# Memory keys of a decoder block: two columns in parts against four columns in native fp32

## The chip, the cores and the metric

The kernel runs on one core of one Trainium2 chip. The metric is the device time of one execution in microseconds; a kernel is run several times and the median is taken. One execution was profiled, and every row below that begins with a time, an engine or a tile comes from its page or its trace.

## The reference

One layer of a decoder: an input projection that feeds a convolution branch and a sparse attention branch, then cross attention over 256 fixed memory tokens, then an MLP. The change touches the keys of the cross attention:

```
memn = _rmsnorm(mem, norm_mem_g)          # mem: 256 tokens x 1024
kv   = memn @ wx_kv                       # 1024 x (512 keys + 512 values)
k, v = jnp.split(kv, 2, axis=-1)          # k: 4 heads x 128
s    = jnp.einsum('bshd,bmhd->bhsm', q, k) * 128 ** -0.5
```

The per-token factor of the norm is applied later, to the scores; here the memory, transposed, is only multiplied by the gain `norm_mem_g`. All data are float32, x has 256 rows, and the model width is 1024, that is eight row tiles of 128 (kt 0 to 7).

## The kernel before

**Products in parts.** Nearly all products are made in parts: a float32 matrix is divided into `hi` (rounded to the fp32r type, by ACT) and `lo` (the rest, by DVE), and TensorE multiplies hi by hi, hi by lo and lo by hi in fp32r. A weight comes as a chunk of 128 x 2048 float32 (1 MB) in the order of the list `STREAM`; `load` issues its transfer on SP's queue, `split_high` and `split_low` take the next half chunk through `high` (ACT, `hi<-raw`) and `low` (DVE, `lo<-raw,hi`). Three buffers hold raw chunks; a new chunk is loaded when the parts of an old one are made. `tile_b` multiplies one column tile of a weight by x or memory; in its `wide` form hi meets both parts side by side (512 columns), then lo meets hi (256).

**A planner in the program.** `Counted` adds up a price of every instruction for TensorE, DVE and ACT. Where work is to be mixed, the generator compares these totals: taps of the convolution are filled into DVE (`meanwhile`, `tick`, `fill_one`) while DVE's total is less than 400 ns ahead of TensorE's (`AHEAD`). `may_fill` says when: with two or more lists of taps always, with one list while more than five tiles are done or while `nused[0] < 5`, the number of weight halves used so far. At the end of the opening all three totals are set to the largest of them.

**The opening**, which the change rewrites, in the order of the program:

- SP: the first half of memory (`mem_t`, row tiles 0 to 3, 512 KB), the first key column (`load_keys(0)`, 512 KB), the second half of memory, the second key column, then the two blocks of x (`x_rm`, 128 rows each) before the halves of the second key chunk (columns 2 and 3), then the first conv chunk in two halves, the conv taps `cw` and the second conv chunk. ACT's queue brings `vec`, the gains and biases.
- TensorE warms up with ten products of zeros, 128 x 512 (`ps_warm`).
- Memory is scaled by its gain on DVE, one instruction for each row tile. Columns 0 and 1 of the keys are multiplied natively in fp32 from the raw chunk, all eight row tiles of one column and then of the other. In between memory is also divided into parts (`mk2`: ACT `mk<-mem_t`, DVE `mk<-mem_t,mk`).
- `square_rows` takes the mean square of a block of x on ACT, a power on GpSimd, and scales the rows on DVE.
- Columns 2 and 3 are divided into parts and multiplied in the wide form, `tile_b(psk[0], ...)` and `tile_b(psk[1], ...)`. Between the two, TensorE transposes x, 16 products into four banks `pt_n` of PSUM (the tag `acc`, which has four).
- `scaled_parts` makes the parts of n out of these banks in the order `BY_BANK`: hi on ACT (`n<-pt_n,vec`), lo on DVE (`n<-pt_n,vec,n`).
- The finished keys are copied to `kx` by ACT; for columns 2 and 3 ACT copies one half of the bank and DVE adds the other (`total`).

Then `conv_in` begins. Its first tile takes a bank through `ps_turn`, whose first turn is the tag `acc`, that is the bank of the first transposes, row tiles 0 and 1:

```
BY_BANK = (0, 2, 4, 6, 1, 3, 5, 7)
tags, turns = [("mm", 2), ("acc", 4)], [0]
def ps_turn(name):
    turns[0] += 1
    tag, bufs = tags[turns[0] % len(tags)]
```

Later in the program memory is loaded once more and divided into parts for the values (`memory_parts`); that is not changed.

Of the kernel before, what the change touches and what calls it, by code (L numbers as in the profile page):

```python
# [8 lines left out]
F32 = mybir.dt.float32  # L9
# [7 lines left out]
P = 128  # L17
# [92 lines left out]
def block_kernel(ctx, tc, x, xt, mem, memt, wst, wki, vecs, convw, gout, out):  # L110
# [21 lines left out]
    def w2(name, dt=F32, shape=(P, 512)):  # L132
        return work.tile(list(shape), dt, tag="w2", bufs=8, name=name)
# [4 lines left out]
    def ps_mm(name):  # L138
        return bank("mm", 2, name)
# [53 lines left out]
    def load(cuts=(0, N_CHUNK), before=lambda q: None, second=False):  # L193
        if not any(by_blocks(key) == second for key in toload):
            return
        key = toload.pop(next(j for j, key in enumerate(toload) if by_blocks(key) == second))
        c = STREAM.index(key)
        raw = t8(f"raw{c}", F32, (P, N_CHUNK)) if c in EARLY or second else raws.tile([P, N_CHUNK], F32, tag="raw", name=f"raw{c}")
        n = KT * NK if key[0] == "ki" else N_CHUNK
        src = wki if key[0] == "ki" else wst[INDEX[key]]  # L200
        for q, ns in enumerate(slice(a, min(b, n)) for a, b in zip(cuts, cuts[1:])):
            before(q)
            nc.sync.dma_start(raw[:, ns], src[:, ns])
            dma[0] += 1.3 * (ns.stop - ns.start)
        if key[0] == "f2" and key[1] < SEVEN:
            seven_factors(key[1], c, raw, dma[0] + LANDED)
            return
        parts = 1 if key[0] == "ki" else 2
        turns = sorted(range(parts), key=lambda q: (*key, q) not in BY_DMA)
        for q in turns:  # L210
            ns = slice(q * n // parts, (q + 1) * n // parts)
            high_jobs.append((lambda ns=ns, q=q, last=q == turns[-1]: high(key, c, raw, ns, q, last), 1, 0, (lambda t=dma[0] + LANDED: t) if key[0] in ("f1", "f2") else None, c))

    def load_keys(q):
        if q == 0:
            toload.pop(0)
            whole["xk", 0] = raws.tile([P, N_CHUNK], F32, tag="raw", name="raw0").rearrange("p (k n) -> p k n", k=2 * KT)
        src = wst[INDEX["xk", 0]].rearrange("p (k n) -> p k n", k=2 * KT)
        nc.sync.dma_start(whole["xk", 0][:, q * KT : q * KT + KT, :], src[:, q * KT : q * KT + KT, :])

    def high(key, c, raw, ns, q, last):
        n = ns.stop - ns.start
# [91 lines left out]
    def split_low():  # L314
        if low_jobs:
            low_jobs.pop(0)()
# [95 lines left out]
    def split(hi, lo, src):  # L412
        act(hi, src, AF.Copy)
        dve.tensor_tensor(out=lo, in0=src, in1=hi.bitcast(F32), op=ALU.subtract)
# [67 lines left out]
    mem_t = t8("mem_t")  # L482
    x_rm = t8("x_rm", F32, (P, 2, D))

    def load_rows(q):
        nc.sync.dma_start(x_rm[:, q, :], x[q * P : (q + 1) * P, :])

    for q in range(2):
        ks = slice(4 * q, 4 * q + 4)
        nc.sync.dma_start(mem_t[:, ks, :], memt[:, ks, :])  # L490
        load_keys(q)
    load((0, 1024, 2048), load_rows)
    load((0, 1024, 2048))
    nc.sync.dma_start(cw, convw.rearrange("p (k t) -> p k t", k=KT))
    load()
    zero = w2("zero")
    nc.vector.memset(zero, 0.0)
    zero_r = cst.tile([P, 512], F32R, name="zero_r")
    nc.vector.tensor_copy(zero_r, zero)
    ident = cst.tile([P, P], F32, name="ident")  # L500
    make_identity(nc, ident)
# [8 lines left out]
    nc.scalar.activation(half, half, AF.Sigmoid, bias=0.0, scale=0.0)  # L510
    nc.gpsimd.memset(half, -0.5)
    ps = ps_aux("ps_warm")
    for j in range(10):
        nc.tensor.matmul(ps, zero_r[:, :P], zero_r, start=True, stop=True)


    def power(ms, name):
# [35 lines left out]
    ss = small.tile([P, 2], F32, tag="ss", name="ss_n")  # L553
    ptn = [ps_acc(f"pt_n{c}") for c in range(4)]

    mk2 = Pair("mk")
    psk = [ps_mm(f"ps_xk0{ct}") for ct in range(2)]
    for ct in range(2):
        for q in range(2):
            for kt in range(4 * q, 4 * q + 4):  # L560
                if ct == 0:
                    dve.tensor_scalar(mem_t[:, kt, :], mem_t[:, kt, :], g_mem[:, kt : kt + 1], None, ALU.mult)
                pe.matmul(psk[ct][:, :S], whole["xk", 0][:, ct * KT + kt, :], mem_t[:, kt, :], start=kt == 0,
                          stop=kt == KT - 1)
            if ct == 0:
                for kt in range(4 * q, 4 * q + 4):
                    split(mk2.hi(kt), mk2.lo(kt), mem_t[:, kt, :])
    load()

    def square_rows(rb):  # L570
# [5 lines left out]
        dve.tensor_scalar(x_rm[:, rb, :], x_rm[:, rb, :], rs[:, 0:1], None, ALU.mult)  # L576

    square_rows(0)
    split_high()
    split_low()  # L580
    square_rows(1)
    for ct in range(2):
        act(kx[:, ct, :], psk[ct][:, :S], AF.Copy)
    split_high()
    split_low()
    psk = [ps_aux(f"ps_xk1{ct}") for ct in range(2)]
    nused[0] += 1
    keys = [[w.rearrange("p (k n) -> p k n", k=KT) for w in prepared.pop(("xk", 1, ct))] for ct in range(2)]
    tile_b(psk[0], keys[0], mk2, wide=True)
    for rb in range(2):  # L590
        for kt in range(KT):
            pe.transpose(ptn[kt // 2][:, (kt % 2) * S + rb * P : (kt % 2) * S + rb * P + P],
                         x_rm[:, rb, kt * P : kt * P + P], ident)
    tile_b(psk[1], keys[1], mk2, wide=True)
    split_high()
    split_low()
    for kt in BY_BANK:
        scaled_parts(n2.hi(kt), n2.lo(kt), ptn[kt // 2][:, (kt % 2) * S : (kt % 2) * S + S], g_mix[:, kt : kt + 1])
    nused[0] += 1
    split_high()  # L600
    split_low()
    for ct in range(2):
        total(kx[:, 2 + ct, :], psk[ct])
    while due:
        due.pop(0)()
    split_high()
    pe.total = dve.total = scalar.total = max(pe.total, dve.total, scalar.total)

# [1033 lines left out]
```

## Time and profile before

| | us |
|---|---|
| median of 3 runs | 503.18 (502.93 to 508.85) |
| profiled execution | 502.87 |
| its span | 500.9 |
| TensorE busy | 490.9 (98%) |
| DVE busy | 456.0 (91%) |
| ACT busy | 384.8 (77%) |
| granted TensorE clock | 0.996 of full, mean |

The span begins with the first instruction and ends with the last. In the rows, PE is TensorE's products, PEld its weight loads, DVE, ACT and POOL the other engines, SPq the queue of transfers that SP issues. A timeline row has start, duration, engine, line, operation, output<-input, shapes and count; in brackets the idle time ahead of it and what ended it. A row of transfers has their count, size and the median time from issue to landing. `L91` is the line of the planner's wrapper, so most instructions have it, and tiles tell them apart.

### The profile page before, as it was taken

Reading aid. Unit: us, or ns where it says so; the run is one execution under the profiler, and the core shown is the slowest. Engines: PE = TensorE matmul, PEld = TensorE weight load, DVE = VectorE, ACT = ScalarE, POOL = GpSimd, SP = SyncE. Lnnn points to the kernel's source line nnn. Section 1 sums busy time; section 2 is a strip of 40 time slices with the busy share of each in tenths; the row PEclk is TensorE's granted clock in tenths of the full one; section 3 lists DMA queues with packets and bytes.
Section 4 is the critical chain, followed back from the end, with each engine's and each line's share of the span. In section 5 each row is a group of like instructions: output and inputs, shape, how many; then the busy total and the mean of one; then the engine's idle time right before and its main releaser. Section 6 shows DMA issues by size and latency. Waiting matters only on the chain.

```text
span 500.9 us, 8179 instructions
## 1 busy us (share of the span) xinstructions
PE 490.9 (98%) x3024; PEld 439.8 (88%) x3024; DVE 456.0 (91%) x835; ACT 384.8 (77%) x678; POOL 54.2 (11%) x75
## 2 busy tenths in 40 slices
PE   7999999999999999999999999999999999999994
PEld 6999999888888989888888888998888888889983
DVE  4889999999999999798999995789899999999996
ACT  4877667878879986888667575597889989899763
POOL 0101122233232210000000000000000010000000
PEclk9999999999999999999999999999999999999998
DMA  8968959999999984373756454665868779788502
GB/s 303 388 270 243 259 146 234 228 250 246 315 287 254 266 219 148 129 298 116 261 183 230 138 198 169 253 252 127 287 195 231 212 221 329 198 264 249 169 0 84
DMA packets 22342, 110.81 MB, mean 221 GB/s; under 512 B 2592, under 2 KB 3104, under 8 KB 11936
## 3 DMA queue, kind: packets, MB, share of 16 engines
q1 hardware_dynamic: 14384, 92.98, 52.7%
q0 software_dynamic: 7632, 17.04, 18.6%
q8 instruction: 23, 0.38, 0.3%
q10 hardware_dynamic: 288, 0.28, 0.2%
q14 instruction: 15, 0.12, 0.1%
HBM read 92.21 MB, written 1.05 MB: 186 GB/s over the span
## 4 chain that ended last, share of the span: by engine, by line
PE 88%; DVE 5%; ACT 3%; DMA 1%; issue 1%; SPq 0%; DVEq 0%; ACTq 0%
PE ps_f L91 14%; PE ps_ff L91 11%; PE ps_conv L91 9%; PE ps_ao L91 4%; PE ps_mix L91 4%; PE ps_co L91 4%; PE ps_ga L91 4%; PE ps_k L91 4%; PE ps_gc L91 4%; PE ps_q L91 4%; PE ps_v L91 4%; PE ps_xo L91 3%; PE ps_xq L91 2%; PE ps_qi L91 2%; PE ps_xk L91 2%; PE ps_xv L91 2%
## 5 line engine op out<-in xcount | busy, mean ns | idle before, releaser
L91 DVE TENSOR_TENSOR lo<-raw,hi 128x1024 fp32r<-128x1024 f32 (+1 forms) x151 | 174.7, 1166 | 8.0 <-ACT hi L91 8.0
L91 ACT ACTIVATE hi<-raw 128x1024 fp32r<-128x1024 f32 (+1 forms) x163 | 161.5, 1011 | 9.6 <-DMA raw<-in_wst_dram 6.1
L91 PE MATMUL ps_f<-ff,hi 128*128 128x256 f32 (+1 forms) x432 | 84.2, 303 | 0.0
L91 PEld LDWEIGHTS ps_f<-ff,hi 128*128 128x128 f32 x432 | 70.9, 191 | 4.4
L91 DVE SCALAR_TENSOR_TENSOR acc<-u,cw,acc 128x249 f32<-128x249 f32 (+17 forms) x150 | 62.6, 467 | 0.0
L91 PE MATMUL ps_f<-ff,lo 128*128 128x256 f32 x256 | 61.0, 283 | 0.0
L675 POOL DMA_DIRECT2D added<-prod x41 | 35.7, 870 | 120.5 <-ACT prod L91 52.7
L91 PE MATMUL ps_conv<-n,hi 128*128 128x256 f32 x256 | 46.6, 284 | 0.0
L91 PEld LDWEIGHTS ps_f<-ff,lo 128*128 128x128 f32 x256 | 44.6, 191 | 0.8
L91 PEld LDWEIGHTS ps_conv<-n,hi 128*128 128x128 f32 x256 | 39.9, 192 | 0.8 <-issue 0.7
L91 DVE TENSOR_TENSOR raw<-raw 128x512 f32<-128x512 f32 (+1 forms) x42 | 36.4, 867 | 0.9
L91 PE MATMUL ps_ff<-th,fs 128*128 128x512 f32 x112 | 36.9, 391 | 0.0
L91 PE MATMUL ps_ff<-hi,fs 128*128 128x512 f32 (+1 forms) x116 | 36.6, 377 | 0.0
L91 PE MATMUL ps_conv<-n,lo 128*128 128x256 f32 x128 | 36.2, 283 | 0.0
L91 ACT ACTIVATE prod<-u,cw 128x226 f32<-128x226 f32 (+10 forms) x82 | 35.0, 475 | 0.8 <-DMA added<-prod 0.8
L91 DVE TENSOR_TENSOR tl<-raw,th 128x1024 fp32r<-128x1024 f32 x28 | 33.2, 1219 | 1.2 <-ACT th L91 1.2
L91 ACT ACTIVATE th<-raw 128x1024 fp32r<-128x1024 f32 x28 | 28.3, 1052 | 1.7 <-DVE raw L91 1.7
L229 POOL DMA_DIRECT2D lo<-raw x12 | 10.4, 866 | 167.1 <-ACT lo L91 110.6
L91 ACT ACTIVATE ft<-ps_f 128x256 f32<-128x256 f32 (+1 forms) x32 | 14.4, 449 | 15.5 <-PE ps_f L91 15.5
L91 PEld LDWEIGHTS ps_ff<-th,fs 128*128 128x128 f32 x112 | 21.1, 188 | 4.2
L91 PEld LDWEIGHTS ps_ff<-hi,fs 128*128 128x128 f32 x116 | 21.4, 189 | 3.6
L91 PEld LDWEIGHTS ps_conv<-n,lo 128*128 128x128 f32 x128 | 24.5, 192 | 0.0
(262 smaller groups left out, 1039.2 us busy)
## 6 DMA issues: line engine op xcount, KB each, us to landing
raw<-in_wst_dram SPq DMA_DIRECT2D x79, 1024.0 KB, 6.2
added<-prod POOLq DMA_DIRECT2D x41, 256.0 KB, 7.7
lo<-raw POOLq DMA_DIRECT2D x12, 512.0 KB, 9.3
raw<-in_wst_dram SPq DMA_DIRECT2D x6, 512.0 KB, 9.3
mem_t<-in_memt_dram SPq DMA_DIRECT2D x2, 512.0 KB, 5.4
x_rm<-in_x_dram SPq DMA_DIRECT2D x2, 512.0 KB, 9.0
mem_rm<-in_mem_dram SPq DMA_DIRECT2D x1, 1024.0 KB, 5.0
mem_t<-in_memt_dram SPq DMA_DIRECT2D x1, 1024.0 KB, 7.0
```

What stands on the lines that cost most here:

```text
L91: return fn(*args, **kwargs)
L229: nc.gpsimd.dma_start(lo.bitcast(F32), raw[:, ns], accum_op=ALU.add)
L675: nc.gpsimd.dma_start(added[:, ts, :].rearrange("p t n -> p (t n)"), prod[:, self.n, :, :].rearrange("p t n -> p (t n)"), accum_op=ALU.add)
```

## The change

`load_keys` takes a column and a range of row tiles instead of a column, and the opening becomes:

- SP: thirteen pieces for memory and all four key columns, 256 KB each but for the first column's low rows, which come as two of 128 KB. The low row tiles (0 to 3) of all columns come first, memory in four pieces among them, then the high row tiles of columns 0 and 1, the two blocks of x, and the high row tiles of columns 2 and 3. The conv chunks and `cw` follow as before.
- Memory is scaled, all eight row tiles, and is not divided into parts. The second key chunk is not divided either.
- TensorE multiplies natively: low rows of columns 0, 1, 2, 3, high rows of columns 0, 1, 2, then the transposes of x, then the high rows of column 3. Columns 2 and 3 use the two `aux` banks.
- ACT copies all four columns to `kx`; the copy of column 2 and `split_high` for the second half of the first conv chunk stand ahead of the parts of n.
- `nused` is not counted up for the second key chunk any more.
- The warm-up is 19 products of 128 x 256, from tiles of zeros of that width.

```diff
-    def load_keys(q):
-        if q == 0:
+    def load_keys(ct, ks):
+        i, ct = divmod(ct, 2)
+        if ("xk", i) not in whole:
             toload.pop(0)
...
+        ks = slice(ct * KT + ks.start, ct * KT + ks.stop)
+        nc.sync.dma_start(whole["xk", i][:, ks, :], src[:, ks, :])
...
-    for q in range(2):
-        ks = slice(4 * q, 4 * q + 4)
+    def load_memory(ks):
         nc.sync.dma_start(mem_t[:, ks, :], memt[:, ks, :])
-        load_keys(q)
-    load((0, 1024, 2048), load_rows)
+
+    low_rows, high_rows = slice(0, 4), slice(4, 8)
+    load_memory(slice(0, 2))
+    load_keys(0, slice(0, 2))
+    load_keys(0, slice(2, 4))
+    load_memory(slice(2, 4))
+    load_keys(1, low_rows)
+    load_keys(2, low_rows)
+    load_memory(slice(4, 6))
+    load_keys(3, low_rows)
+    load_memory(slice(6, 8))
+    for rb in range(2):
+        load_keys(rb, high_rows)
+    for rb in range(2):
+        nc.sync.dma_start(x_rm[:, rb, :], x[rb * P : (rb + 1) * P, :])
+    for ct in range(2, 4):
+        load_keys(ct, high_rows)
     load((0, 1024, 2048))
...
-    zero = w2("zero")
+    zero = cst.tile([P, S], F32, name="zero")
...
-    for j in range(10):
-        nc.tensor.matmul(ps, zero_r[:, :P], zero_r, start=True, stop=True)
+    for j in range(19):
+        nc.tensor.matmul(ps[:, :S], zero_r[:, :P], zero_r, start=True, stop=True)
...
-    mk2 = Pair("mk")
-    psk = [ps_mm(f"ps_xk0{ct}") for ct in range(2)]
...
+    psk = [ps_mm(f"ps_xk{ct}") for ct in range(2)] + [ps_aux(f"ps_xk{ct}") for ct in range(2, 4)]
+    for kt in range(KT):
+        dve.tensor_scalar(mem_t[:, kt, :], mem_t[:, kt, :], g_mem[:, kt : kt + 1], None, ALU.mult)
+
+    def keys(ct, ks):
+        for kt in range(ks.start, ks.stop):
+            pe.matmul(psk[ct][:, :S], whole["xk", ct // 2][:, ct % 2 * KT + kt, :], mem_t[:, kt, :], start=kt == 0,
+                      stop=kt == KT - 1)
+
+    for ct in range(4):
+        keys(ct, low_rows)
+    for ct in range(3):
+        keys(ct, high_rows)
     load()
...
     square_rows(0)
-    split_high()
-    split_low()
     square_rows(1)
     for ct in range(2):
         act(kx[:, ct, :], psk[ct][:, :S], AF.Copy)
     split_high()
     split_low()
...
-    tile_b(psk[0], keys[0], mk2, wide=True)
+    act(kx[:, 2, :], psk[2][:, :S], AF.Copy)
+    split_high()
     for rb in range(2):
         for kt in range(KT):
             pe.transpose(ptn[kt // 2][:, (kt % 2) * S + rb * P : (kt % 2) * S + rb * P + P],
                          x_rm[:, rb, kt * P : kt * P + P], ident)
-    tile_b(psk[1], keys[1], mk2, wide=True)
-    split_high()
-    split_low()
+    keys(3, high_rows)
+    load()
     for kt in BY_BANK:
         scaled_parts(n2.hi(kt), n2.lo(kt), ptn[kt // 2][:, (kt % 2) * S : (kt % 2) * S + S], g_mix[:, kt : kt + 1])
-    nused[0] += 1
-    split_high()
     split_low()
-    for ct in range(2):
-        total(kx[:, 2 + ct, :], psk[ct])
-    while due:
-        due.pop(0)()
+    act(kx[:, 3, :], psk[3][:, :S], AF.Copy)
     split_high()
```

More of the change, by code (lines that the diff above doesn't have):

```diff
@@ L212, in load @@
             high_jobs.append((lambda ns=ns, q=q, last=q == turns[-1]: high(key, c, raw, ns, q, last), 1, 0, (lambda t=dma[0] + LANDED: t) if key[0] in ("f1", "f2") else None, c))
-    def load_keys(q):
-        if q == 0:
+    def load_keys(ct, ks):
+        i, ct = divmod(ct, 2)
+        if ("xk", i) not in whole:
             toload.pop(0)
-            whole["xk", 0] = raws.tile([P, N_CHUNK], F32, tag="raw", name="raw0").rearrange("p (k n) -> p k n", k=2 * KT)
-        src = wst[INDEX["xk", 0]].rearrange("p (k n) -> p k n", k=2 * KT)
-        nc.sync.dma_start(whole["xk", 0][:, q * KT : q * KT + KT, :], src[:, q * KT : q * KT + KT, :])
+            whole["xk", i] = raws.tile([P, N_CHUNK], F32, tag="raw", name=f"raw{i}").rearrange("p (k n) -> p k n", k=2 * KT)
+        src = wst[INDEX["xk", i]].rearrange("p (k n) -> p k n", k=2 * KT)
+        ks = slice(ct * KT + ks.start, ct * KT + ks.stop)
+        nc.sync.dma_start(whole["xk", i][:, ks, :], src[:, ks, :])
     def high(key, c, raw, ns, q, last):
@@ L483, in block_kernel @@
     x_rm = t8("x_rm", F32, (P, 2, D))
-    def load_rows(q):
-        nc.sync.dma_start(x_rm[:, q, :], x[q * P : (q + 1) * P, :])
-    for q in range(2):
-        ks = slice(4 * q, 4 * q + 4)
+    def load_memory(ks):
         nc.sync.dma_start(mem_t[:, ks, :], memt[:, ks, :])
-        load_keys(q)
-    load((0, 1024, 2048), load_rows)
+    low_rows, high_rows = slice(0, 4), slice(4, 8)
[14 more added lines that the diff above has]
+        load_keys(ct, high_rows)
     load((0, 1024, 2048))
@@ L495, in block_kernel @@
     load()
-    zero = w2("zero")
+    zero = cst.tile([P, S], F32, name="zero")
     nc.vector.memset(zero, 0.0)
-    zero_r = cst.tile([P, 512], F32R, name="zero_r")
+    zero_r = cst.tile([P, S], F32R, name="zero_r")
     nc.vector.tensor_copy(zero_r, zero)
@@ L554, in block_kernel @@
     ptn = [ps_acc(f"pt_n{c}") for c in range(4)]
-    mk2 = Pair("mk")
-    psk = [ps_mm(f"ps_xk0{ct}") for ct in range(2)]
-    for ct in range(2):
[L559 to L567, printed above, removed]
+    psk = [ps_mm(f"ps_xk{ct}") for ct in range(2)] + [ps_aux(f"ps_xk{ct}") for ct in range(2, 4)]
[9 more added lines that the diff above has]
+        keys(ct, high_rows)
     load()
@@ L585, in block_kernel @@
     split_low()
-    psk = [ps_aux(f"ps_xk1{ct}") for ct in range(2)]
-    nused[0] += 1
-    keys = [[w.rearrange("p (k n) -> p k n", k=KT) for w in prepared.pop(("xk", 1, ct))] for ct in range(2)]
-    tile_b(psk[0], keys[0], mk2, wide=True)
+    act(kx[:, 2, :], psk[2][:, :S], AF.Copy)
+    split_high()
     for rb in range(2):
@@ L593, in block_kernel @@
                          x_rm[:, rb, kt * P : kt * P + P], ident)
-    tile_b(psk[1], keys[1], mk2, wide=True)
-    split_high()
-    split_low()
+    keys(3, high_rows)
+    load()
     for kt in BY_BANK:
         scaled_parts(n2.hi(kt), n2.lo(kt), ptn[kt // 2][:, (kt % 2) * S : (kt % 2) * S + S], g_mix[:, kt : kt + 1])
-    nused[0] += 1
-    split_high()
     split_low()
-    for ct in range(2):
-        total(kx[:, 2 + ct, :], psk[ct])
-    while due:
-        due.pop(0)()
+    act(kx[:, 3, :], psk[3][:, :S], AF.Copy)
     split_high()
```

## The prediction

> **What bounds the kernel now.** I read the page first, then the table of three stretches of time, then the timeline of TensorE alone up to the first conv product, and after that the other engines around it. The page's head and its engine line:
>
> ```profile
> span 500.9 us, 8179 instructions
> PE 490.9 (98%) x3024; PEld 439.8 (88%) x3024; DVE 456.0 (91%) x835; ACT 384.8 (77%) x678; POOL 54.2 (11%) x75
> ```
>
> The table cuts the span at the first conv product (21.44) and after the last product (493.72); its second and third rows are shown. The columns are the stretch, its length, and each engine's busy time and instructions.
>
> ```profile
> 21.44:493.72 472.28, 472.13 (x2936) 424.01 (x2934) 438.83 (x793) 368.73 (x644) 51.74 (x61) 1.00 0.71 217
> 493.72:500.90 7.18, 0.00 (x0) 0.00 (x0) 3.42 (x12) 2.81 (x8) 0.00 (x0) 0.72 0.40 146
> ```
>
> The first of them decides how to argue. TensorE is busy for 472.13 of 472.28 us, so from the first conv product on nothing waits that an edit ahead of it could relieve. The change lies wholly in the first stretch. Its effect is therefore the move of one moment, the start of conv at 21.44, unless it opens a gap later. That stretch on TensorE (start, duration, operation, count):
>
> ```profile
> 1.92 4.17 PE L514 MATMUL ps_warm<-zero_r 128*128 128x512 f32 x10 [1.92 <-DVE zero_r L499]
> 6.26 1.97 PE L91 MATMUL ps_xk<-mem_t,raw 128*128 128x256 f32 x8 [0.17 <-DVE mem_t L91]
> 8.80 5.45 PE L91 MATMUL ps_xk<-mem_t,raw 128*128 128x256 f32 x24 [0.58 <-DVE mem_t L91]
> ...
> 13.90 2.20 PE L91 MATMUL ps_xk<-mk,hi 128*128 128x512 f32 x8
> ...
> 16.89 1.91 PE L91 MATMUL pt_n<-ident,x_rm 128*128 128x128 f32 x16
> 18.55 2.10 PE L91 MATMUL ps_xk<-mk,hi 128*128 128x512 f32 x8
> ...
> 21.44 0.40 PE L91 MATMUL ps_conv<-n,hi 128*128 128x256 f32 x2
> ```
>
> Two waits stand in it: 0.17 before the first key product and 0.58 before 8.80, where the second half of memory is late. The 16 native products of columns 0 and 1 show as 32 records, two for each. Their spacing comes from two narrower views of the same run of records, of which the first begins 13 records and the second 2 records before its end:
>
> ```profile
> 11.28 2.97 PE L91 MATMUL ps_xk<-mem_t,raw 128*128 128x256 f32 x13
> ...
> 13.66 0.59 PE L91 MATMUL ps_xk<-mem_t,raw 128*128 128x256 f32 x2
> ```
>
> That is 11 records in 2.38 us, 0.216 each.
>
> **The change, part by part.**
>
> TensorE's work. Removed are the two columns in parts: 13.90 to 16.89 is 2.99 us, and 18.55 to 21.44 is 2.89 us. Added are 32 records for each, 16 per column, so 16 x 0.216 = 3.46 us a column. The two columns become 2 x 3.46 - 5.88 = 1.04 us dearer. Against that stand the two waits of 0.17 and 0.58 and an earlier start.
>
> ACT and DVE. Removed are the parts of memory and of columns 2 and 3. By form, within the first 22 us:
>
> ```profile
> L91 ACT ACTIVATE mk<-mem_t 128x256 fp32r<-128x256 f32 x8 | 2.7, 405 | 4.8 <-DVE mem_t L91 4.8
> L91 DVE TENSOR_TENSOR mk<-mem_t,mk 128x256 fp32r<-128x256 f32 x8 | 2.8, 413 | 0.0
> L91 ACT ACTIVATE hi<-raw 128x1024 fp32r<-128x1024 f32 x4 | 4.2, 1070 | 0.1
> L91 DVE TENSOR_TENSOR lo<-raw,hi 128x1024 fp32r<-128x1024 f32 x3 | 3.6, 1211 | 0.0
> L91 DVE SCALAR_TENSOR_TENSOR n<-pt_n,vec,n 128x256 fp32r<-128x256 f32 x8 | 3.2, 475 | 0.0
> ```
>
> That spares ACT 2.7 + 2 x 1.07 = 4.8 us and DVE 2.8 + 2 x 1.21 = 5.2 us, and two adds. By itself it is worth nothing, since TensorE stood behind neither of them after 8.80; it counts only where it lets something start earlier. The scaling of memory stays.
>
> Start of the key products. They need the constants (vec), the first piece of memory, the first key piece and the end of the warm-up.
>
> ```profile
> mem_t<-in_memt_dram SPq DMA_DIRECT2D x1, 512.0 KB, 4.1
> vec<-in_vecs_dram ACTq DMA_DIRECT2D x1, 36.0 KB, 4.3
> ...
> raw<-in_wst_dram SPq DMA_DIRECT2D x1, 512.0 KB, 4.9
> ...
> 5.06 1.14 DVE L91 TENSOR_SCALAR mem_t<-mem_t,vec 128x256 f32<-128x256 f32 x4 [3.19 <-DMA vec<-in_vecs_dram]
> 8.40 1.14 DVE L91 TENSOR_SCALAR mem_t<-mem_t,vec 128x256 f32<-128x256 f32 x4 [0.86 <-DMA mem_t<-in_memt_dram]
> ```
>
> The issues of memory and vec at 0.74 and 0.75 landed at 4.9 and 5.05, and DVE starts at 5.06. From DVE's start to the product is 0.40 (8.40 to 8.80), which gives 5.46. Of the warm-up, 19 x 256 columns against 10 x 512 is 4.17 x 0.95 = 3.96 us; its start moves from 1.92 to about 1.6, since the two tiles of zeros ahead of it are half as wide, so it ends at 5.4 to 5.7. I take 5.5 for the first key product; bounds are 5.3 (vec earlier) and 5.75 (start of the warm-up unmoved).
>
> Memory's second piece. Before, 512 KB were there at 4.9 and 1 MB (with the first key column, issued at 1.18) at 6.1. The new second piece ends 768 KB: 5.5, between 4.9 and 6.1. It is needed 0.40 ahead of the fifth record, 5.5 + 0.9 - 0.4 = 6.0. So it does not stop TensorE, by half a microsecond. All later key and memory pieces have more: the last memory piece ends 2 MB, which before landed at 9.6 (one step of 1.28 ahead of x's first block, below), and is used after 12.
>
> The queue. Eight SP transfers up to the last key column become 15. Their issues take SP about 0.45 each (three in 1.47, a wait included). SP holds back after the eighth transfer, and each later one waits for the landing of the one eight places before it (5.05 behind vec, 8.39 behind memory's second half):
>
> ```profile
> 5.05 1.47 SPq L203 DMA_DIRECT2D raw<-in_wst_dram  x3
> 8.39 0.33 SPq L494 DMA_DIRECT2D cw<-in_convw_dram  x1
> ```
>
> Eight pieces of 256 KB are 2 MB in flight, 5 us of transfers, so the engines are not starved. The runs of memory and of a key column per partition halve, 4 KB to 2 KB. The nearest row for that is the ki transfer with runs of 2304 bytes; the first row is a half microsecond of it alone, the second is of 4-KB runs:
>
> ```profile
> DMA packets 92, 0.19 MB, mean 387 GB/s; under 512 B 8, under 2 KB 8, under 8 KB 92
> ...
> DMA packets 575, 2.09 MB, mean 419 GB/s; under 512 B 64, under 2 KB 64, under 8 KB 575
> ```
>
> 3.1 MB at 387 instead of 419 GB/s are 0.6 us more; the bounds are 0 and, for the two 128-KB pieces with runs half as long again, 0.8. What is later by that: the rows of x and the first conv weights. Before:
>
> ```profile
> x_rm<-in_x_dram SPq DMA_DIRECT2D x1, 512.0 KB, 8.2
> ...
> x_rm<-in_x_dram SPq DMA_DIRECT2D x1, 512.0 KB, 9.7
> ...
> raw<-in_wst_dram SPq DMA_DIRECT2D x1, 512.0 KB, 11.2
> ...
> 13.49 1.06 ACT L91 ACTIVATE junk_x_rm<-x_rm 128x1024 bf16<-128x1024 f32 x1 [0.22 <-DMA x_rm<-in_x_dram]
> 14.55 0.64 ACT L91 ACTIVATE kv<-ps_xk 128x256 f32<-128x256 f32 x2
> 15.08 2.04 ACT L91 ACTIVATE hi<-raw 128x1024 fp32r<-128x1024 f32 x2
> 18.18 3.03 ACT L91 ACTIVATE n<-pt_n,vec 128x256 fp32r<-128x256 f32 x8 [1.06 <-PE pt_n L91]
> ...
> 15.64 0.81 DVE L91 TENSOR_SCALAR x_rm<-x_rm,rs_n 128x1024 f32<-128x1024 f32 x1 [0.67 <-POOL rs_n L575]
> 18.68 3.22 DVE L91 SCALAR_TENSOR_TENSOR n<-pt_n,vec,n 128x256 fp32r<-128x256 f32 x8
> ```
>
> The first block of x (issue 2.67 + 8.2) landed at 10.9 and the second (3.81 + 9.7) at 13.5, with one piece of 512 KB between them: 1.28 us a piece. The second has the same 3.5 MB up to its end as before, so 14.1; it is normalised 3.0 later (13.5 to 16.45), at 17.1. The second half of the first conv weights (issue 6.14 + 11.2 = 17.3) comes at 17.9.
>
> The Trainium skill speaks against small pieces: "DMA: Bandwidth & Descriptors" gives about 2 us of fixed cost to each transfer (section "Anatomy of one DMA") and asks for 1 MiB or more to reach three quarters of the peak (section "Bandwidth"). In this trace 512-KB pieces land 1.28 us apart, so with eight in flight that cost is overlapped. By the rule taken piece by piece, 256 KB would cost an estimated 2.6 us each, x's second block would come after more than 30 us and the sum would be some 20 us higher; by the rows it is 0.6 us of transfer.
>
> The end of the stretch. Low rows of four columns and high rows of three stand ahead of the transposes: 56 records x 0.216 = 12.1, plus 0.1 for the slower first record. The transposes start at 5.5 + 12.2 = 17.7; x is there at 17.1. They take 1.66 (16.89 to 18.55), the last half column 8 x 0.216 = 1.73, and TensorE is free for conv at 21.1. But before, 4.55 us lay between the start of the transposes and conv, filled by a whole column in parts (2.89); now the cover is 1.73. What comes out from under it is the way of n: conv's first bank is that of the first transposes, and is free only after the fifth DVE instruction of n (order 0, 2, 4, 6, 1). From ACT's first n to that: 0.50 (18.18 to 18.68), four spacings of 0.39 ((3.22 - 0.48) / 7), and 0.48, with the hand-over 2.6. ACT's first n was 1.29 behind the transposes, which would give 17.7 + 1.29 + 2.6 = 21.6. And ahead of n ACT now has the copy of column 2, which waits for that column's end (17.7 + 0.2: the record begun at 13.66 + 0.22 ended at 14.25, 0.16 past its spacing; then 0.27, as two copies take 0.64), and hi of the second conv half (0.97, landed at 17.9): 19.1. So conv starts at 19.1 + 2.6 = **21.7** instead of 21.44, a loss of 0.26. Behind it DVE ends n at 19.6 + 3.2 = 22.8 and lo of the second conv half at 24.0; the second conv tile needs that at 21.7 + 2.88 (23.04 us for eight tiles, below) = 24.6.
>
> Moved loads. The conv weights 2 and 3 are issued behind column 1 and column 3, near 16.3 and 21.5. One such transfer of 1 MB took
>
> ```profile
> raw<-in_wst_dram SPq DMA_DIRECT2D x1, 1024.0 KB, 10.5
> ...
> 21.60 23.04 PE ps_conv L91 x192
> ```
>
> 10.5 us, at worst landing at 32; the chain has four pairs in 23.04, so weights 3 are needed at 21.7 + 3 x 5.76 = 39. Hidden.
>
> The sum: 0.26 later. The profiled execution took 502.87 (2.0 around its span) and becomes 503.1. The median of the runs is 0.3 above it, so **503.4 us**.
>
> **The rivals.**
>
> TensorE alone decides (not slower): should conv's first product not wait for the transposes' bank, it starts when TensorE is free, 21.1, a gain of 0.34, and 502.8 us. For it speaks that nothing stopped conv before; against it that 0.66 of slack (18.18 + 2.6 = 20.8 against 21.44) was all there was, and ACT's first n moves by more.
>
> Late pieces (slower): the small transfers come later than a shared stream would bring them. It decides from 6.0 for memory's second piece, 14.7 for x and 18.1 for the second conv half. Before, the second half of memory was the slow one, 6.7 us after its issue:
>
> ```profile
> mem_t<-in_memt_dram SPq DMA_DIRECT2D x1, 512.0 KB, 6.7
> ```
>
> It ended 1.5 MB, the new second piece ends 0.75 MB, three half steps less: 6.7 - 1.9 = 4.8. Issued fourth, at 2.1, it would land at 6.9, 0.9 late, and all behind it moves along: conv at 22.6, 504.3 us. Against it: x and the conv weights of before came in even steps. The Trainium skill's rule of the fixed cost, above, points to this rival.
>
> Taps ahead of splits (slower): the planner lets a single list of taps be filled while fewer than five weight halves are used, and that count now starts two lower. Up to 19 taps of the first tile could then come before weight parts on DVE:
>
> ```profile
> L91 DVE SCALAR_TENSOR_TENSOR acc<-u,cw,acc 128x249 f32<-128x249 f32 (+17 forms) x150 | 62.6, 467 | 0.0
> ```
>
> 19 x 62.6 / 150 = 7.9 us, of which the pair split ahead covers 5.76: at most 2.2, 505.6 us. Against it: the planner lets taps run only 0.4 us of its own count ahead of TensorE.
>
> The change does little for what it spares: that is part of the forecast, since no one waited for ACT and DVE.
>
> **How the numbers follow.** Forecast 0.5; TensorE alone 0.2; late pieces 0.2; taps 0.05; 0.05 for more than one of these. The range is 502.4 to 504.8: below, the gain of 0.34 with the earlier start of 5.3 (another 0.2) and the spread of the runs; above, late pieces and 0.5 of spread. All of it lies far inside 2% (10 us), which is about what a measurement of this kernel tells from no change: faster 0.01, within 0.98, slower 0.01.
>
> **What would show it.** Right: 64 native records 0.216 apart without a gap above 0.1 from about 5.5, transposes near 17.7, hi of the second conv half directly ahead of the first n, a TensorE wait of about 0.6 behind the last half column put down to n on DVE, conv near 21.7, and TensorE unbroken to the end. Wrong: conv before 21.3, a wait among the key products, or a TensorE gap after conv has begun.

## The result, and the profile after

The changed kernel took 509.87 us (median of 6 runs, 508.96 to 510.94) against 503.19 for the kernel before: ratio 1.0130, 95% interval 1.0106 to 1.0155. The forecast was 503.4 with a range up to 504.8, so it was wrong by 6.5 us, on the slower side; that the change would stay inside 2% held. The profiled execution took 509.36.

The head and the engine line of the page after:

```profile
span 507.6 us, 8181 instructions
PE 493.3 (97%) x3033; PEld 441.8 (87%) x3033; DVE 451.2 (89%) x823; ACT 379.8 (75%) x668; POOL 55.6 (11%) x75
```

The span is 6.7 longer, and DVE and ACT are busy for 5 us less each: what the change spared them was spared, and the span did not shorten by it. The table of stretches, cut as before at the first conv product (now 24.15) and after the last product (now 499.85):

```profile
24.15:499.85 475.70, 472.67 (x2934) 423.96 (x2934) 439.60 (x792) 367.87 (x644) 53.09 (x61) 1.00 0.71 215
499.85:507.60 7.75, 0.00 (x1) 0.00 (x0) 3.42 (x12) 2.81 (x8) 0.00 (x0) 0.79 0.37 136
```

So the loss comes in three parts: 2.71 before conv starts (24.15 against 21.44), 3.42 in the middle (475.70 against 472.28) and 0.57 in the tail (7.75 against 7.18). The middle was to be untouched. TensorE's waits from 20 us on:

```profile
PE ps_rsb L91 <- POOL rs_vr L532: 1.8, 1, 1.8
PE ps_conv L91 <- DVE n L91: 1.3, 1, 1.3
PE ps_co L91 <- DVE u L91: 1.1, 1, 1.1
```

The second is the forecast one, of the transposes' bank (forecast at 0.6, now 1.27). The first and the third lie 200 us behind the edit, in and behind the norm of the conv branch. Nothing like them stood there before; they make 2.9 of the 3.42, and the rest is 0.54 more of busy time (472.67 against 472.13), which I did not follow.

**The opening, after.** TensorE's timeline:

```profile
5.73 1.18 PE L91 MATMUL ps_xk<-mem_t,raw 128*128 128x256 f32 x4
7.29 4.58 PE L91 MATMUL ps_xk<-mem_t,raw 128*128 128x256 f32 x20 [0.38 <-DVE mem_t L91]
12.26 7.14 PE L91 MATMUL ps_xk<-mem_t,raw 128*128 128x256 f32 x32 [0.39 <-DMA raw<-in_wst_dram]
19.24 1.91 PE L91 MATMUL pt_n<-ident,x_rm 128*128 128x128 f32 x16
20.99 1.89 PE L91 MATMUL ps_xk<-mem_t,raw 128*128 128x256 f32 x8
24.15 0.51 PE L91 MATMUL ps_conv<-n,hi 128*128 128x256 f32 x2 [1.27 <-DVE n L91]
```

The chain of work that leads to the end of the opening (start, duration, what):

```profile
4.38 7.74 DMA raw<-in_wst_dram
...
12.14 7.17 DMA raw<-in_wst_dram
...
19.33 1.06 ACT hi L91
20.39 0.27 ACT kv L91
20.66 0.99 ACT hi L91
21.65 0.37 ACT n L91
...
22.05 2.06 DVE n L91 x5
...
24.15 23.29 PE ps_conv L91 x192
```

Read from below, this is the way of n as forecast: five DVE instructions of n, ACT's first n, ahead of it hi of the second conv half and the copy of column 2. But it does not begin at a product. It begins at two transfers: a key piece that landed at 12.12, and behind it (SP issues it at 12.14, when that key piece, eight places before it, has landed) the first half of the conv weights, which landed at 19.31. Both halves were there at 16.03 and 17.34 before, at 19.31 and 20.57 now. The forecast gave the second 17.9, and no time to the first. ACT takes the two halves in order, so n comes behind both:

```profile
21.56 3.01 ACT L91 ACTIVATE n<-pt_n,vec 128x256 fp32r<-128x256 f32 x8
```

The transfers of the stretch from 5 to 11 us in the kernel before, then after:

```profile
DMA packets 615, 2.23 MB, mean 371 GB/s; under 512 B 71, under 2 KB 71, under 8 KB 615
```

```profile
DMA packets 866, 1.58 MB, mean 264 GB/s; under 512 B 94, under 2 KB 94, under 8 KB 866
```

The DMA engines were at work for 0.93 of that stretch (0.99 before), so they were not short of work; each packet took longer for its bytes (estimate: 103 ns of an engine for 1.8 KB, 155 ns for 3.6 KB before). From 11 to 16 us they moved 405 and 411 GB/s.

**The norm, after.** The kernel before, then after: TensorE's sums and factors of the conv branch's norm.

```profile
207.33 0.60 PE L91 MATMUL ps_mub<-usum,onesd 128*128 128x256 f32 x2
219.39 0.38 PE L91 MATMUL ps_rsb<-ident,rs_vr 128*128 128x128 f32 x2
```

```profile
215.73 0.59 PE L91 MATMUL ps_mub<-usum,onesd 128*128 128x256 f32 x2
229.71 0.43 PE L91 MATMUL ps_rsb<-ident,rs_vr 128*128 128x128 f32 x2 [1.76 <-POOL rs_vr L532]
```

The sums come 8.40 later, of which conv's start explains 2.71. They add up the finished taps. Taps are shared between DVE (`acc<-u,cw,acc`) and 41 products that ACT makes and that accumulating transfers of POOL's queue add to `added`. POOL's issues of these, before:

```profile
36.60 1.04 POOL L675 DMA_DIRECT2D added<-prod  x1 [20.70 <-ACT sg L91]
43.93 0.88 POOL L675 DMA_DIRECT2D added<-prod  x1 [6.29 <-ACT prod L91]
...
183.12 0.86 POOL L675 DMA_DIRECT2D added<-prod  x1 [3.15 <-ACT qk L91]
```

and after:

```profile
40.42 1.04 POOL L679 DMA_DIRECT2D added<-prod  x1 [21.17 <-ACT sg L91]
51.36 0.87 POOL L679 DMA_DIRECT2D added<-prod  x1 [9.90 <-ACT qi_t L91]
...
191.80 0.86 POOL L679 DMA_DIRECT2D added<-prod  x1 [5.01 <-ACT prod L91]
```

The first is 3.8 late, the second 7.4 and the last 8.7: a place in the order was lost between the first and the second, and was not made good. At the same time DVE began its taps earlier. Its first, before and after:

```profile
34.70 0.61 DVE L91 TENSOR_SCALAR acc<-u,cw 128x255 f32<-128x255 f32 x2
```

```profile
31.67 0.35 DVE L91 TENSOR_SCALAR acc<-u,cw 128x255 f32<-128x255 f32 x1
```

### The profile page after: what moved, and what is told of

Its sections match the earlier page's. It is cut to its first block, busy times and chain, and to the rows that moved or that the text cites. A ratio compares the mean times of both kernels' runs of the same rounds, so it can differ in the third digit from the quotient of the medians.

```text
span 507.6 us, 8181 instructions
## 1 busy us (share of the span) xinstructions
PE 493.3 (97%) x3033; PEld 441.8 (87%) x3033; DVE 451.2 (89%) x823; ACT 379.8 (75%) x668; POOL 55.6 (11%) x75
## 4 chain that ended last, share of the span: by engine, by line
PE 79%; DVE 9%; ACT 6%; DMA 4%; issue 1%; POOL 0%; DVEq 0%; ACTq 0%
PE ps_f L91 14%; PE ps_ff L91 11%; PE ps_conv L91 9%; PE ps_mix L91 4%; PE ps_k L91 4%; PE ps_gc L91 4%; PE ps_q L91 4%; PE ps_v L91 4%; PE ps_ga L91 4%; PE ps_co L91 4%; PE ps_xo L91 3%; DMA raw<-in_wst_dram 3%; ACT hi L91 2%; PE ps_xq L91 2%; PE ps_qi L91 2%; DVE lo L91 2%
## 5 line engine op out<-in xcount | busy, mean ns | idle before, releaser
L91 DVE TENSOR_TENSOR lo<-raw,hi 128x1024 fp32r<-128x1024 f32 (+2 forms) x149 | 172.4, 1165 | 7.9 <-ACT hi L91 7.9
L91 ACT ACTIVATE hi<-raw 128x1024 fp32r<-128x1024 f32 (+2 forms) x161 | 159.4, 1009 | 12.2 <-DMA raw<-in_wst_dram 6.7
L91 DVE SCALAR_TENSOR_TENSOR acc<-u,cw,acc 128x253 f32<-128x253 f32 (+18 forms) x150 | 63.1, 467 | 0.2
```

Source lines behind the costliest of these rows:

```text
L91: return fn(*args, **kwargs)
```

## The experiments

**What was to be told apart.** For the middle: theory A, that the planner's count `nused`, which the change leaves two lower, reorders taps and products, against the view that the late opening itself is what comes out again at the norm. For the opening: whether the price is the late transfers (and if so their run length, their number, or the size of memory's or the keys' pieces), the bank of the transposes, or TensorE's own dearer work. Ratios are to the kernel before, run beside each on the same chip; they lie near the ratio of the mean times, so a few long runs of the kernel before lower them, and the text goes by medians.

| run | us, median (runs) | ratio, 95% interval | conv starts |
|---|---|---|---|
| before | 503.19 (6) | | 21.44 |
| after | 509.87 (6) | 1.0130, 1.0106 to 1.0155 | 24.15 |
| e1 | 505.20 (10) | 1.0030, 1.0013 to 1.0047 | 23.33 |
| e2 | 506.29 (6) | 1.0057, 1.0030 to 1.0084 | 21.56 |
| e3 | 509.51 (1) | | 22.81 |
| e4 | 508.46 (1) | | 23.80 |
| e5 | 505.17 (8) | 1.0047, 1.0031 to 1.0063 | 22.14 |
| e6 | 504.79 (10) | 1.0041, 1.0020 to 1.0062 | 22.71 |
| e7 | 504.33 (12) | 1.0026, 1.0011 to 1.0041 | 22.53 |
| e8 | 504.45 (9) | 1.0025, 1.0015 to 1.0035 | 22.54 |
| e9 | 504.67 (1) | | 22.50 |
| e10 | 510.36 (1) | | 28.53 |
| e11 | 502.51 (11) | 0.9983, 0.9966 to 0.9999 | 21.37 |
| e12 | 509.27 (1) | | 26.16 |

### The count given back (e1) and taken away (e2)

e1 is the changed kernel with the two counts that the opening no longer makes put back at its end; e2 is the kernel before with the counts taken away there, and nothing else.

```diff
+    nsplit[0] += 2
+    nused[0] += 2
```

```diff
+    nsplit[0] -= 2
+    nused[0] -= 2
```

> The changed kernel, with the planner's two counters (nsplit, nused) raised by 2 where the opening ends, so that the count of used weight halves is the one of before; nothing else. Theory A (the loss has two parts: conv starts 2.7 us later, and the lower count reorders the taps, so that one accumulating transfer of the convolution comes a turn later and the layer norm, and with it the product behind it, is awaited by TensorE): conv still starts near 24.1, but the waits of TensorE near 228 (1.8) and 241 (1.1) are gone and the time is before + 2.7 to 2.9, 505.6 to 506.2 us. Rival B (the waits at 228 and 241 come from the late opening itself): they stay and the time stays near 509.5.

> The kernel before, with both counters lowered by 2 at the end of the opening; nothing else, the opening is the old one. Theory A: conv starts at 21.4 as before, waits of TensorE of 1 to 2 us each appear behind the layer norm near 225 and 238, and the time is before + 3.3 to 3.9, 506.5 to 507.1 us. Rival B: no change, 503.2 us.

e1 brought the changed kernel from 509.87 to 505.20; e2 took the kernel before from 503.15 (its 15 runs beside e1 and e2) to 506.29. The norm in e1, then in e2:

```profile
209.32 0.60 PE L91 MATMUL ps_mub<-usum,onesd 128*128 128x256 f32 x2
221.38 0.38 PE L91 MATMUL ps_rsb<-ident,rs_vr 128*128 128x128 f32 x2
```

```profile
214.80 0.59 PE L91 MATMUL ps_mub<-usum,onesd 128*128 128x256 f32 x2
228.79 0.43 PE L91 MATMUL ps_rsb<-ident,rs_vr 128*128 128x128 f32 x2 [1.77 <-POOL rs_vr L519]
```

In e1 all of it is 1.99 behind the kernel before, which is nearly its conv start (1.89 later), and no wait is left. In e2 conv starts on time and the norm comes late with the same wait of 1.77, and a wait of 1.1 behind it. (e2's profile also has a wait of 1.5 for `ps_s`; its profiled run was 507.99, above its median.) So theory A holds, in both directions: two units of a counter are worth 3.1 us in the kernel before (506.29 - 503.15). A late opening alone does not bring the wait: in e10 and e12 below conv starts at 28.53 and 26.16 with the counts of before, and TensorE does not wait at the norm.

The two parts do not quite add up in the medians. e1 still stands 2.0 behind its own kernel before (505.20 - 503.15), and with the 3.1 that makes 5.2 of the 6.7. In the changed kernel the count is worth 4.7 (509.87 - 505.20): in the profiles 3.3 of it lie behind conv's start, and conv also starts 0.82 earlier, which the edit cannot cause. The rest was not followed.

The way goes so, by the program. With `nused` two lower when conv begins, `may_fill` lets the first list of taps go to DVE at once: the first tap is at 31.67 instead of 34.70. The queue of low parts is then one longer, ACT's planned total is further ahead, and at the turn where the second accumulating product is due ACT counts as too busy; it is passed over and made two turns later. A group issues only one accumulating transfer at a time, so each of its later ones moves back one place, the second half of the taps is added two turns later, and the norm, which TensorE met ready in the kernel before, is late. This was read from the lists that the program writes, not from the trace. With the counters moved by two, the order that the program writes out for taps, products and halves is the same as before's. The traces agree as far as they show it: in e1 the first four accumulating transfers are issued 1.9 to 2.0 behind those of the kernel before, no place lost there.

### The pieces merged (e3, e4)

Both are the changed kernel: e3 loads memory in two pieces of 512 KB, e4 loads the same row tiles of two key columns in one transfer of 512 KB (two runs of 2 KB a partition), and memory's third piece moves ahead of the second key transfer.

```diff
-    load_memory(slice(0, 2))
+    load_memory(low_rows)
...
-    load_memory(slice(2, 4))
...
-    load_memory(slice(4, 6))
+    load_memory(high_rows)
...
-    load_memory(slice(6, 8))
```

```diff
+        w, src = (a.rearrange("p (c k) n -> p c k n", c=2)[:, :, ks, :] for a in (whole["xk", i], src))
+        nc.sync.dma_start(w, src)
...
-    load_keys(0, slice(0, 2))
-    load_keys(0, slice(2, 4))
+    load_keys(0, low_rows)
...
```

> The changed kernel with memory in two transfers of 512 KB (runs of 4 KB per partition) instead of four of 256 KB, the key pieces as they are. Theory M (each packet of memory is slow to read, about 60 ns whatever its size, and four pieces have twice as many): the landing of the first conv half moves from 19.3 to about 18.3 and conv starts about 1 us earlier than 24.1. Theory S (it is the number and size of transfers in flight): two of seventeen transfers fewer, the first conv half lands within 0.4 of 19.3 and conv moves by no more than 0.4.

> The changed kernel with the key pieces in pairs, two columns in one transfer of 512 KB (four transfers instead of nine; the runs stay at 2 KB), memory in its four pieces. Theory S (transfers in flight: eight of 256 KB hold too little when one of the sixteen engines lags): the stretch from 5 to 11 us moves clearly more than the 240 GB/s of the changed kernel, the first conv half lands before 18.3, conv starts at 23.2 or earlier. Theory M (packets of memory): the landing stays within 0.4 of 19.3.

The first conv half landed at 17.93 in e3 and 17.97 in e4, against 19.31; from 5 to 11 us they moved 317 and 332 GB/s, against 264 (the 240 of e4's expectation). The 60 ns a packet of theory M stand in no run. Four profiles whose transfers are the same (after, e1, e5, e6) have 264, 261, 279 and 276 GB/s, and the landing at 19.31, 18.46, 18.83 and 18.04. So the higher rate of either merge is beyond the scatter, and the gain in the landing hardly is. Each was run once. As far as that goes, the slowness belongs neither to memory's pieces alone nor to the keys' alone. The total time did not follow in e3, which has a further wait of 1.1 for `ps_s` and the norm's two waits; e4 gave part of the gain back at its start, since the first product waits for a larger piece (6.67).

e3 also shows what the late conv weights cost by themselves. Its key products run without a gap from 5.47 and the transposes start at 17.95, a quarter of a microsecond behind the forecast. Conv still starts only at 22.81, because ACT makes hi of both conv halves (from 17.95) before the first n (20.22).

### The way of n (e5, e6)

Both stand on e1. e5 lets conv's first tile take another bank than that of the first transposes; e6 puts hi of the second conv half behind the parts of n.

```diff
-    tags, turns = [("mm", 2), ("acc", 4)], [0]
+    tags, turns = [("mm", 2), ("acc", 4)], [1]
```

```diff
     act(kx[:, 2, :], psk[2][:, :S], AF.Copy)
-    split_high()
...
     for kt in BY_BANK:
         scaled_parts(n2.hi(kt), n2.lo(kt), ptn[kt // 2][:, (kt % 2) * S : (kt % 2) * S + S], g_mix[:, kt : kt + 1])
+    split_high()
     split_low()
```

> The changed kernel with the counters back (as e1) and with the turn of the banks begun one later, so that conv's first tile takes a bank of the finished keys instead of the bank of the first transposes. Theory C (conv's start is set by that bank, free only after five instructions of n on DVE, behind hi of the second conv half on ACT, which waits for its landing): conv starts when TensorE is free, 22.0 instead of 23.3, the wait of 1.3 goes, and the time is 1.0 to 1.4 below e1, 503.8 to 504.2 us. Rival D (conv waits for the landing of the conv weights or for n itself): conv stays at 23.0 or later, 505.0 us or more.

> The changed kernel with the counters back (as e1) and hi of the second conv half moved behind the parts of n on ACT. Theory C: ACT's first n no longer waits for the landing of that half (19.7 in e1) but for the transposes, 1.3 behind their start, and conv starts about 0.9 earlier than in e1, near 22.4: 504.1 to 504.6 us. Rival E (x or the transposes are what ACT's n waits for anyway): no change, 505.2 us.

In e5 conv follows the last half column at once:

```profile
20.60 1.89 PE L91 MATMUL ps_xk<-mem_t,raw 128*128 128x256 f32 x8
22.14 0.60 PE L91 MATMUL ps_conv<-n,hi 128*128 128x256 f32 x2
```

```profile
26.00 0.38 PE L91 MATMUL ps_conv<-n,lo 128*128 128x256 f32 x1 [0.39 <-DVE lo L91]
```

So the bank was what conv waited for. But the next wait is close behind: the second conv tile wants lo of the late second half, and the medians of e5 and e1 are equal (505.17 and 505.20), so the 503.8 to 504.2 of theory C did not come. Of the 1.19 by which conv starts earlier than in e1, that wait takes 0.39, and at the norm's sums 0.4 is left (208.9 against 209.3); what took the rest was not followed. In e6 the wait for n shrinks from 1.16 to 0.27 and conv starts at 22.71; the median is 0.4 lower, which the intervals do not tell from e1. There ACT's n waits for the transposes instead (18.81, first n at 20.10). Taking the chain apart at either place brought 0.4 us at most in the medians, with the conv weights and the key pieces as late as they were.

### TensorE's own work (e7, e8)

e7 is the native keys with the transfers of before: eight pieces of 512 KB in the old order, whole columns 0, 1 and 2, the transposes, column 3, the counters as before. e8 is e7 with the other bank.

```diff
+    load_memory(low_rows)
+    load_keys(0, rows)
+    load_memory(high_rows)
+    load_keys(1, rows)
     for rb in range(2):
         nc.sync.dma_start(x_rm[:, rb, :], x[rb * P : (rb + 1) * P, :])
...
+        load_keys(2 + rb, rows)
...
     for ct in range(3):
-        keys(ct, high_rows)
+        keys(ct, rows)
...
```

> The native products of all four key columns alone: the eight transfers of the kernel before in their old sizes and order, each column multiplied whole (0, 1, 2, then the transposes, then 3), counters as before. Theory F (the native products cost nothing by themselves, the pieces are what is late): conv starts at 21.4 to 21.6, 503.0 to 503.4 us. Rival G (native fp32 is dearer by the 1.04 us of TensorE and shows it): conv at 22.2 or later, 504.0 us or more.

> e7 with the banks of e5. Theory C: conv starts when TensorE is free, near 20.9, 0.5 before e7 and before the kernel before: 502.4 to 502.8 us, faster than both. Rival: the same as e7, since the way of n has slack with the old transfers.

TensorE in e7:

```profile
8.78 8.90 PE L91 MATMUL ps_xk<-mem_t,raw 128*128 128x256 f32 x40 [0.57 <-DVE mem_t L91]
17.52 1.91 PE L91 MATMUL pt_n<-ident,x_rm 128*128 128x128 f32 x16
19.27 3.62 PE L91 MATMUL ps_xk<-mem_t,raw 128*128 128x256 f32 x16
22.53 0.59 PE L91 MATMUL ps_conv<-n,hi 128*128 128x256 f32 x2
```

There is no gap from 8.78 to conv, which starts 1.09 later than before; the forecast's 1.04 for the dearer columns is there in full, and the median is 1.25 above the kernel before, as rival G expected. The expectation that it would be hidden was a mis-sum: 56 records from 8.78 at 0.216 and 1.66 of transposes end at 22.5. e8 is the same (22.54, 504.45) and not the 502.4 to 502.8 of its theory C, since with timely weights the way of n has slack under the whole last column. Of e7's runs the profiled one took 505.74, 1.4 above the median, with an extra wait of 0.9 for `ps_pt`. The new warm-up stands in both, and the first key product starts at 6.25 and 6.27, against 6.26 before: no price of it shows.

### Run length or number of transfers (e9, e10, e12)

All three are the kernel before with only its first eight transfers rewritten; the diffs show the lines for memory, those for the keys and x are like them. e9 cuts each along the row: 16 of 256 KB with runs of 2 KB. e10 cuts each along the partitions: 16 of 256 KB, 64 partitions each, runs of 4 KB. e12 keeps eight of 512 KB, but each made of two runs of 2 KB a partition. R in the expectations puts the cost on the length of a run, N on the number of transfers.

```diff
...
+            kh = slice(ks.start + 2 * h, ks.start + 2 * h + 2)
+            nc.sync.dma_start(mem_t[:, kh, :], memt[:, kh, :])
...
```

```diff
...
+            ps = slice(64 * h, 64 * h + 64)
+            nc.sync.dma_start(mem_t[ps, ks, :], memt[ps, ks, :])
...
```

```diff
...
+        m, src = (a.rearrange("p (a b c) n -> p b a c n", a=2, b=2)[:, q] for a in (mem_t, memt))
+        nc.sync.dma_start(m, src)
...
```

> The kernel before with each of its first eight SP transfers (memory, two key columns, x, the second key chunk) cut in two along the row, so that sixteen transfers of 256 KB with runs of 2 KB stand in the old order; products as before. The first conv half landed at 16.0 before, and at 18.0 to 19.3 in the four profiles of the changed kernel's transfers. Theory R (runs of 2 KB): it lands at 17.2 or later. Theory N (twice the transfers, eight in flight): the same here, and the same in the next run. Theory Z (the changed order, memory and keys in turn): it lands before 16.6.

> The kernel before with the same eight transfers cut in two along the partitions: sixteen transfers of 256 KB, 64 partitions each, runs of 4 KB as before. Theory R (runs of 2 KB): the first conv half lands near 16.0 to 16.6. Theory N (number and size of transfers): it lands at 17.2 or later.

> The kernel before with its eight transfers kept at 512 KB and in their order, but each made of two runs of 2 KB per partition instead of one of 4 KB (memory row tiles 0, 1, 4, 5 and then 2, 3, 6, 7; key pieces for two columns at once; x by column halves); products unchanged. Theory R (runs of 2 KB slow the reading): from 5 to 11 us about 320 GB/s as in e9, not 371, and the first conv half lands at 17.0 or later. Theory N (sixteen transfers with eight in flight slow it): 360 GB/s or more, and the first conv half at 16.0 to 16.6.

Transfers from 5 to 11 us, in e9, e10 and e12:

```profile
DMA packets 1052, 1.91 MB, mean 319 GB/s; under 512 B 118, under 2 KB 118, under 8 KB 1052
```

```profile
DMA packets 408, 1.33 MB, mean 222 GB/s; under 512 B 83, under 2 KB 83, under 8 KB 408
```

```profile
DMA packets 1056, 2.04 MB, mean 340 GB/s; under 512 B 60, under 2 KB 60, under 8 KB 1056
```

Against 371 in the kernel before, runs of 2 KB cost 14% (e9) and 8% (e12) in this stretch; the first conv half landed at 18.14 and 18.86 instead of 16.03. e12 has as few transfers as before and lands no earlier than e9 with twice as many, and the number of packets that got through is the same (1056 and 1052). That speaks for R, and so does e11 below, where only the four key pieces have runs of 2 KB: 361 GB/s. It is no clean proof. e12's rate lies between the two expectations, both were run once, and SP took longer to issue e12's transfers (the eighth at 6.88, against 5.05 in the kernel before), so that part of its late landing is late issue.

e10 says nothing on this question. Its landing, near 24.0, is by the letter what N expected, but it brought a disturbance of its own: 222 GB/s, and 234 from 11 to 16 us where e9 has 368 and e12 399, with the engines at work all the time. The Trainium skill, "DMA: Bandwidth & Descriptors" (section "Rules for kernel authors"), advises against two transfers to disjoint halves of the partitions and says that they serialize. The trace agrees with the advice: the rate of e10 is little more than half. The reason given, that both halves use the same engines, would by itself leave the sum of the two at the full rate; why it fell stays open here.

e12's 509.27 is not the price of the runs, either. With the two columns side by side in each piece the first key product has to wait for a later landing, and the granted clock is 0.52 for the next 3.4 us. TensorE's first products, and a table of the stretches around them (length, busy time, granted clock, DMA share, GB/s):

```profile
9.38 9.18 PE L91 MATMUL ps_xk<-mem_t,raw 128*128 128x256 f32 x32 [3.09 <-DMA raw<-in_wst_dram]
```

```profile
5.90:9.38 3.48, 0.39 (x2) 0.98 1.00 310
9.38:12.80 3.42, 3.42 (x8) 0.52 1.04 398
12.80:18.50 5.70, 5.64 (x26) 1.00 1.06 408
```

### Low rows first, the rest left in parts (e11)

The one part of the change that the runs had not spoken against, alone on the kernel before: low row tiles of columns 0 and 1 before the high ones, key pieces of 256 KB behind each half of memory; columns 2 and 3 still in parts, the counters untouched.

```diff
...
-        load_keys(q)
+        load_keys(0, ks)
+        load_keys(1, ks)
...
-    for ct in range(2):
-        for q in range(2):
+    for q in range(2):
+        for ct in range(2):
...
```

> The kernel before with the low row tiles of columns 0 and 1 first (memory in its two halves, the key pieces 256 KB each, products low rows of 0 and 1, then high rows); columns 2 and 3 stay in parts. If the late second half of memory is all that stops TensorE in the opening, the wait of 0.58 at 8.80 goes and conv starts 0.5 to 1.0 earlier, 20.4 to 20.9: 502.1 to 502.6 us, faster than both. If small key pieces delay memory's second half as they did in the changed kernel, conv starts at 21.4 or later: 503.1 us or more.

```profile
5.97 7.38 PE L91 MATMUL ps_xk<-mem_t,raw 128*128 128x256 f32 x32
13.91 2.14 PE L91 MATMUL ps_xk<-mk,hi 128*128 128x512 f32 x8 [0.56 <-ACT hi L91]
...
21.37 0.44 PE L91 MATMUL ps_conv<-n,hi 128*128 128x256 f32 x2
```

502.51 against 503.00 (15 runs beside it): ratio 0.9983, interval 0.9966 to 0.9999. It is faster than both kernels, by half a microsecond in the medians: nine of its 11 runs lie below the lowest of the 15 (502.79). The key products run from 5.97 without the wait of 0.58, and then the first product in parts waits for hi of column 2. So conv starts 0.07 earlier and not the 0.5 to 1.0 expected, and its profile does not show where the half microsecond comes from.

## Why the prediction was wrong, step by step

- **"so from the first conv product on nothing waits that an edit ahead of it could relieve", and from this that the effect is "the move of one moment, the start of conv at 21.44".** This is the step that failed by most. A stretch in which TensorE is busy for 472.13 of 472.28 us shows that nothing can be gained there. It doesn't show that nothing can be lost: the norm's work on DVE and POOL had less slack than one place in the order is worth, and no view of TensorE's waits shows slack. The sum had no term for such a gap; its "unless it opens a gap later" was priced only in the rival of the taps. Price: 3.1 (e2, in the medians), 3.42 in the profile after.
- **"Taps ahead of splits", chance 0.05, at most 2.2.** It names the right cause, the count two lower, and looked for the price in the wrong place: taps delaying weight parts on DVE at the start. The taps did start 3.0 earlier (31.67), and no weight part was missed. The price came near 229 and 242 us, from accumulating products that came a place later; that one was passed over is read from the program. That "the planner lets taps run only 0.4 us of its own count ahead" was no argument against it: a reordered list cost more here than the time by which it runs ahead. The range also left out the 505.6 of this rival.
- **Runs of 2 KB: "3.1 MB at 387 instead of 419 GB/s are 0.6 us more", at most 0.8.** The mechanism was seen and mis-sized. The second conv half landed at 20.57 instead of the forecast 17.9, that is 2.7 beyond. The price was read from a row at 33 us (387 against 419 GB/s); from 5 to 11 us the rate was 264 against 371. Since hi of both conv halves stands ahead of n, nearly all of the lateness went into n: ACT's first n at 21.56 against 19.1. The late transposes alone would have put it near 20.5 (19.24 + 1.29).
- **Memory's second piece at 5.5.** It landed at 6.85. The rival "late pieces" had worked out 4.8 us from its issue and 6.9, and this happened as well: TensorE waited at 7.29, and once more, for a key piece, at 12.26. Transposes began at 19.24 instead of 17.7. A wait among the key products and a gap behind conv's start were two of the forecast's own signs of being wrong.
- **The Trainium skill's rule against small pieces** (prediction, above) pointed the right way; twenty microseconds was far off, as the rows had said. The page fits its fixed cost to transfers that GpSimd issues, and these were issued by SP. What e9, e11 and e12 suggest is that here the length of a run counts, more than the number of transfers by which the rule prices them.
- **Right:** the native records' 0.216 and the 1.04 of dearer work (1.09 in e7); the first product at 5.5 (5.73, within its bounds, but held by the warm-up, which took 4.42 and not 3.96; vec had landed at 4.36); the bank as the thing conv waits for (e5), with five DVE instructions of n and 2.6 from ACT's first n to conv (21.56 to 24.15); hi directly ahead of n; that what ACT and DVE are spared brings nothing (e7).

The opening adds up. From 5.73, 56 records and the slow first (12.2), transposes (1.66) and the last half column (1.73) would end at 21.32. Waits and slowed records up to the transposes add 1.31 (19.24 - 17.93), the transposes 0.09, the bank 1.43: 24.15. Of the 6.7 in the span, 2.71 is this, 3.42 the count, and 0.57 is the tail behind the last product, which no run was aimed at. It is not bound to the change: over the profiles it is 7.1 to 7.8, and e9 and e10, with the old products, have 7.7.

What stays open: why 2-KB runs move at 264 GB/s in the changed kernel and at 319 in e9, in the same stretch. e3 and e4 suggest that memory's and the keys' pieces share in it, no more. Open too are the 1.5 us by which the two parts miss the whole in the medians.

## What to carry to other kernels

A kernel whose program plans its own order by counts has an interface that no engine's time shows: when an edit removes work, look for every counter that work moved, and keep them or replan, because the list of instructions far behind the edit may change. A saturated engine is proof against gains, not against losses; ask for each late join (a norm, an accumulation) how early its inputs are, not only whether it waits now. Take the price of a transfer from rows of the same moment of the program, with the same neighbours on the queue.

## What the runs showed of the hardware

- Engines at work for 0.90 to 1.01 of the time didn't mean one rate from 5 to 11 us: 371 to 380 GB/s with runs of 4 KB (before, e2, e7, e8), 361 where only four pieces had runs of 2 KB (e11), 261 to 340 where more of them or all had (after, e1, e3 to e6, e9, e12). From 11 to 16 us these runs moved 368 to 413 with either.
- Transfers to 64 of the 128 partitions ran at 222 to 234 GB/s from 5 to 16 us, with the engines fully at work (e10).
- A TensorE that had waited 3.09 us ran the next 3.42 us at a granted clock of 0.52 (e12, above). One that had waited 2.51 us had a mean of 0.56 over the next 3.51 us (e10; length, busy time, granted clock, DMA share, GB/s):

```profile
8.79:12.30 3.51, 3.51 (x9) 0.56 1.04 237
```

  Cut finer, the fall is not tied to the restart. In both runs TensorE stopped at 6.3 us, the granted clock was 1.00 up to 9.2 and 0.50 from 9.3 to 12.6, and was back at 1.00 by 12.7. By 9.2 TensorE had been at work again for 0.4 us in e10, and was still waiting in e12.

  The Trainium skill, "TensorE: Matmul & The Clock Gate" (Part 1), has the clock fall to half after an idle window of about 3.4 us, and return after about as long at work. The half clock and its length agree; the idle time that sufficed here was shorter, 2.51 us in e10.
